# Grouping the products of the state steps and the attention by shape, and a new order for both

## The chip, the cores and the metric

One core of a Trainium2 chip. The metric is the device time of one execution in microseconds, the median of three runs. PE is TensorE, DVE is VectorE, ACT is ScalarE, POOL is GpSimd, SP is SyncE (here it only issues DMAs). PE's granted clock is 2.4 GHz where the profile shows 1.00 and 1.2 GHz where it shows 0.50.

## What the kernel computes

Two residual layers over 512 tokens of 1024 values. The change lies in the mixer of layer 0, which has eight heads of RWKV-7 and eight heads of stick-breaking attention, all 64 wide:

```
def step(S, inp):                                   # RWKV-7, one token
    r_t, w_t, k_t, v_t, a_t, b_t = inp
    sa = jnp.einsum('bhvk,bhk->bhv', S, a_t)
    S = S * w_t[:, :, None, :] + sa[..., None] * b_t[:, :, None, :] + v_t[..., None] * k_t[:, :, None, :]
    return S, jnp.einsum('bhvk,bhk->bhv', S, r_t)
...
for blk in range(t_len // SB_BLOCK):                # attention, 128 queries at a time
    z = jnp.einsum('bhqd,bhkd->bhqk', q[:, :, q0:end], k[:, :, :end]).astype(jnp.float32) * scale
    log_1m_beta = jnp.where(causal, jax.nn.log_sigmoid(-z), 0.0)
    after = lax.cumsum(log_1m_beta, axis=3, reverse=True) - log_1m_beta
    att = jnp.where(causal, jnp.exp(jax.nn.log_sigmoid(z) + after), 0.0)
    outs.append(jnp.einsum('bhqk,bhkd->bhqd', att.astype(v.dtype), v[:, :, :end]))
```

Before it comes the input projection, behind it the output projection, a mixture of 16 experts, layer 1 and another mixture.

## The kernel before, in words

The projections leave everything on the chip, then `values` prepares the RWKV part and the stage of this change begins: the state steps and the attention, woven into each other on PE, ACT and DVE. Two heads form a pair, 128 partitions, so there are four pairs in either part.

**The steps.** The 512 tokens are cut into 8 chunks of 64, and `step(c)` carries the state over one chunk for all pairs at once. It is a chain: `p1` multiplies the old state (L612), `d1` adds to it on DVE (L615), `p2` multiplies by a 128x128 inverse (L621), `a2` copies the result out of PSUM in two halves on ACT (L625), `p3` makes the new state (L630), which `d3` scales on DVE (L634, L635), and `p4` makes the output (L641, L643), which `a4` copies out (L646). The chain to the next step goes p2, a2, p3, d3, p1, d1. In `p1` and `p2` a product has 128 weight columns and 64 moving columns, one for each pair. In `p4` each pair has two products with all 128 rows and 64 columns of weights (L641) and two, for the old state, with 64 rows and 64 columns (L643), in turns.

**The attention.** A pair's 8 query blocks are packed into 5 units of 512 columns (`attend(k)`, pair k // 5, unit k % 5). A unit goes through `z` (scores on PE, L755, and a mask added as a product of an identity with a triangle of -1e30, L756), `a1` to `a3` on ACT (Abs, Exp, Ln), `d1` (DVE, L772), `d2` (running sums on DVE, one for each query block, L779), `d3` (DVE, scores less sums, L782), `t` (four transposes on PE, L786), `a4` (Exp on ACT, L790) and, for three of the five, `av` (weights times values, L804). Scores of units 1 to 4 are three products of split numbers (high x high, low x high, high x low) over a head's 64 rows; a unit of one head uses one half of PE's rows. `cut_qk` makes the split for the next pair, on ACT and POOL (L296, L297).

**What sets the order.** `even` gives each part a time from the tables STEP, UNIT, OUT and SPLIT, plus 2 * ITER = 16.4 for each pair, sorts the parts and issues them in that order; PE, ACT and DVE run their instructions in it, each engine by itself, with semaphores between. The tables are numbers of a plan, not times of the chip.

```
at = p * 2 * ITER
parts = [(at + t, f) for t, f in zip(UNIT[j], (z, a1, a2, a3, d1, d2, d3, t, a4, av))]
...
for _, f in sorted(parts, key=lambda x: x[0]):
    f()
```

Behind the stage comes `a_out` (16 products of 128x512 for the RWKV heads: L663, L671, L681, L682), then `out_proj`, whose weights and residual rows SP loads during the stage (L820, L951) as buffers come free.

Of the kernel before, what the change touches and what calls it, by code (L numbers as in the profile page):

```python
# [12 lines left out]
AF = mybir.ActivationFunctionType  # L13
OP = mybir.AluOpType
# [4 lines left out]
T = 512  # L19
# [24 lines left out]


ITER = 8.2
STEP = (dict(p1=1.45, d1=1.90, p2=2.59, a2=5.24, p3=5.37, d3=5.86, p4=10.90, a4=17.57),
        dict(p1=7.47, d1=8.81, p2=9.34, a2=10.12, p3=12.64, d3=14.66, p4=14.62, a4=18.80))
UNIT = ((0.00, 1.87, 4.48, 5.31, 5.68, 6.60, 6.64, 8.13, 9.59, 20.86),
# [4 lines left out]
OUT = 27.10, 37.12  # L54
SPLIT = 12.74


class Arena:
# [100 lines left out]
class Kern:  # L159
# [180 lines left out]
    def consts_even(self):  # L340
        nc, ar = self.nc, self.ar

        self.bo = ar.get(128)
        self.bo64 = ar.get(128)
        for b, v in ((self.bo, 1.0), (self.bo64, 1.0 / 64)):
            nc.gpsimd.memset(b.f(), 0.0)
            for s in range(2):
                nc.gpsimd.memset(b.f()[s * 64:s * 64 + 64, s * 64:s * 64 + 64], v)

        self.cm = ar.get(128)  # L350
        nc.gpsimd.memset(self.cm.f(), 1.0)
        for s in range(2):
            v = self.cm.f()[s * 64:s * 64 + 64]
            nc.gpsimd.affine_select(v[:, 0:64], v[:, 0:64], [[1, 64]], OP.is_gt, 0.0, base=0, channel_multiplier=-1)
            nc.gpsimd.affine_select(v[:, 64:128], v[:, 64:128], [[1, 64]], OP.is_ge, 0.0, base=0, channel_multiplier=-1)

        self.atc = ar.get(128)
        self.identb, self.late = self.atc.b(2, 128)[:, 0], self.atc.b(2, 128)[:, 1]
        nc.gpsimd.tensor_copy(self.identb, self.ident)
        nc.gpsimd.memset(self.late, 0.0)  # L360
        nc.gpsimd.affine_select(self.late, self.late, [[-1, 128]], OP.is_gt, -1e30, base=0, channel_multiplier=1)

        self.sm = ar.get(T)
        nc.gpsimd.memset(self.sm.f(), 1.0)
        nc.gpsimd.memset(self.sm.f(8, 64)[:, :, 0:1], 0.0)
# [226 lines left out]
    def step(self, c):  # L592


        nc, ar = self.nc, self.ar
        UV, AR = self.UV.f(8, 4, 2, 64), self.AR.f(4, 8, 3, 64)
        XI, RV, BT, MR = self.AMa.f(4, 8, 128), self.RV.f(4, 8, 64), self.BT.f(4, 8, 128), self.AMr.f(4, 8, 2, 64)
        S, old = [self.S[(c + i) % 2].f(4, 64) for i in range(2)]
        R1 = self.R1.f(4, 64)
        both = lambda a: a.rearrange("p s v -> p (s v)")  # L600
        q = [slice(s * 64, s * 64 + 64) for s in range(2)]
        pairs = [(p, s) for p in range(4) for s in range(2)]
        B = {}
# [12 lines left out]

        def p2():
            b = bank(2)
            rhs = R1 if c else RV[:, :, c]
            for p in range(4):  # L620
                nc.tensor.matmul(b[:, p], XI[:, p, c], rhs[:, p], start=True, stop=True)  # L621

        def a2():
            for s in range(2):
                nc.scalar.activation(UV[q[s], c, :, s], B[2][q[s]], AF.Copy)  # L625

        def p3():
            b = bank(3)
            for p, s in pairs:
                nc.tensor.matmul(b[q[s], p], BT[:, p, c, q[s]], UV[:, c, p, s], start=True, stop=True)  # L630

        def d3():
            if c:
                nc.vector.tensor_tensor(S, B[3], old, OP.add)  # L634
            nc.vector.tensor_tensor(S, S if c else B[3], self.LC.f(4, 8)[:, :, c:c + 1].to_broadcast([128, 4, 64]), OP.mult)  # L635

        def p4():
            b = bank(4)
            for p in range(4):
                for s in range(2):  # L640
                    nc.tensor.matmul(b[q[s], p], UV[:, c, p, s], MR[:, p, c, s], start=True, stop=not c)  # L641
                for s in range(2 if c else 0):
                    nc.tensor.matmul(b[q[s], p], old[q[s], p], AR[q[s], p, c, 2], start=False, stop=True, tile_position=(s * 64, s * 64))  # L643

        def a4():
            nc.scalar.activation(AR[:, :, c, 2], B[4], AF.Copy)  # L646

        parts = dict(p1=p1, d1=d1, p2=p2, a2=a2, p3=p3, d3=d3, p4=p4, a4=a4)
        skip = ("p1", "d1") if not c else ("p3", "d3") if c == 7 else ()
        return [(c // 2 * 2 * ITER + STEP[c % 2][n], f) for n, f in parts.items() if n not in skip]  # L650

# [79 lines left out]
    def attend(self, k):  # L731


        nc = self.nc
        p, j = divmod(k, 5)


        unit = ([(0, 1, 0), (1, 1, 256)], [(0, 3, 0)], [(1, 3, 0)], [(0, 2, 0), (0, 0, 384)], [(1, 2, 0), (1, 0, 384)])[j]
        N = 512
        B = {}  # L740

        def z():
            z = self.bank(("pj", "at")[k % 2])
            for s, qb, c in unit:
                hs, n = slice(s * 64, s * 64 + 64), qb * 128 + 128
                terms = [(self.QK[p].f(2, T), self.QK[p].f(2, T))]
                if not j:

                    hs, terms = slice(0, 128), [(self.QZ.f(2, 1, 128)[:, s], self.QK[p].f(2, T))]
                elif qb:  # L750
                    h, l = self.whi.bufs[p % 2].r(2, T), self.wlo.bufs[p % 2].r(2, T)
                    terms = [(h, h), (l, h), (h, l)]
                q = slice(qb * 128, n) if j else slice(0, 128)
                for i, (a, b) in enumerate(terms):
                    nc.tensor.matmul(z[:, c:c + n], a[hs, 0, q], b[hs, 1, 0:n], start=not i, stop=i == len(terms) - 1)  # L755
                nc.tensor.matmul(z[:, c + n - 128:c + n], self.identb, self.late, start=False, stop=True, skip_group_check=True)  # L756
            if not j and p < 3:
                self.beside(p + 1)
            B["z"], B["s"] = z, self.spq.next().f()


        def a1():
            nc.scalar.activation(B["s"], B["z"], AF.Abs)

        def a2():
# [3 lines left out]
            self.after(nc.scalar.activation(B["s"], B["s"], AF.Ln, bias=self.eps[:, 2:3]))  # L769

        def d1():
            nc.vector.scalar_tensor_tensor(B["s"], B["z"], 0.0, B["s"], OP.max, OP.add)  # L772


        def d2():
            for s, qb, c in unit:
                n = qb * 128 + 128
                v = _back(B["s"][:, c:c + n])
                nc.vector.tensor_tensor_scan(v, self.eps[:, 2:3].to_broadcast([128, n]), v, 0.0, OP.mult, OP.add)  # L779

        def d3():
            nc.vector.tensor_tensor(B["s"], B["z"], B["s"], OP.subtract)  # L782

        def t():
            for i in range(0, N, 128):
# [1 line left out]

        def a4():
            w = self.rsr.next().f()
            self.after(nc.scalar.activation(w, B["z"], AF.Exp))  # L790
            self.w[k] = w, unit

        def av():
# [11 lines left out]
                                     self.VT[p].f(4, 128)[:, kb, s * 64:s * 64 + 64], w, start=kb == 0, stop=kb == qb)  # L805

        at = p * 2 * ITER
        parts = [(at + t, f) for t, f in zip(UNIT[j], (z, a1, a2, a3, d1, d2, d3, t, a4, av))]
        if not j and p < 3:
            parts.append((at + SPLIT, lambda: self.cut_qk(p + 1)))  # L810
        if j == 4:
            parts += [(at + t, f) for t, f in zip(OUT, self.out_in(4 + p, lambda: self.o))]
        return parts
# [90 lines left out]
    def even(self):  # L904
        nc, ar, I = self.nc, self.ar, self.I
# [43 lines left out]
        x = I["x"].rearrange("b (t p) d -> p (b t) d", p=128)  # L949
# [724 lines left out]
```

## Time and profile before

| | us |
|---|---|
| median of 3 runs (1259.72 to 1261.07) | 1260.58 |
| the profiled execution, device time | 1263.75 |
| its span in the profile | 1262.0 |
| PE busy over the span | 1195.3 |
| DVE, ACT, POOL busy | 1027.3, 800.2, 486.4 |

The busy time of PE is modelled, so that 95% says only that PE seldom stands without an instruction. The trace numbers microseconds from the start of the span; the stage of this change runs from 250.91, when the first `p2` begins, to 338.35, when the last `av` ends.

### The profile page before, as it was taken

How to read it: one execution, taken by the hardware profiler on the slowest of the kernel's cores; microseconds unless marked ns; L12 is line 12 of the kernel's file. 1: busy time of each engine (PE TensorE's matmuls, PEld its weight loads, DVE VectorE, ACT ScalarE, POOL GpSimd, SP SyncE). 2: the span in 40 equal slices, each digit the busy share in tenths (PEclk: the TensorE clock that was granted, in tenths of full speed). 3: DMA queues.
4: the chain of work that ended last, by engine and by line, in shares of the span. 5: the costliest groups of instructions: out<-in, count | busy, mean ns of one | idle time of the engine just before them, and what ended most of it. 6: DMA issues, size and time to landing. Idle time of an engine off the chain costs nothing. (4 is left out here: it accounts for less than half of the span.)

```text
span 1262.0 us, 18000 instructions
## 1 busy us (share of the span) xinstructions
PE 1195.3 (95%) x6602; PEld 880.3 (70%) x6603; DVE 1027.3 (81%) x1316; ACT 800.2 (63%) x1071; POOL 486.4 (39%) x321
## 2 busy tenths in 40 slices
PE   6999998999999799999999899999997999999997
PEld 5777765877678477777777676677775777777764
DVE  4387899567776899999998665599657999999985
ACT  6533332367744588888888564475445888888883
POOL 8043200201011246667775301120113466667753
PEclk9999999979999899999999999999998999999998
DMA  6312221001776889999997532256678999999964
GB/s 167 84 50 67 67 67 34 2 18 43 258 245 232 311 293 361 356 346 357 351 365 265 155 87 67 68 174 239 221 247 277 327 367 369 350 345 347 352 223 145
DMA packets 152390, 274.46 MB, mean 217 GB/s; under 512 B 8171, under 2 KB 59052, under 8 KB 152294
## 3 DMA queue, kind: packets, MB, share of 16 engines
q1 hardware_dynamic: 142438, 247.85, 57.1%
q0 software_dynamic: 7840, 18.04, 6.1%
q10 hardware_dynamic: 2016, 7.34, 1.4%
q8 instruction: 54, 0.88, 0.3%
q14 instruction: 42, 0.34, 0.1%
HBM read 258.80 MB, written 22.28 MB: 223 GB/s over the span
## 5 line engine op out<-in xcount | busy, mean ns | idle before, releaser
L296 ACT ACTIVATE R<-A 128x1024 fp32r<-128x1024 f32 (+1 forms) x451 | 473.2, 1053 | 206.3 <-PE ps_pj L1350 68.0
L297 DVE TENSOR_TENSOR R<-A,R 128x1024 fp32r<-128x1024 f32 (+1 forms) x362 | 493.7, 1397 | 77.9 <-ACT R L296 73.9
L297 POOL TENSOR_TENSOR R<-A,R 128x1024 fp32r<-128x1024 f32 x89 | 257.1, 2889 | 292.7 <-ACT R L296 288.6
L1351 PE MATMUL ps_pj<-R 128*96 128x512 f32 x512 | 205.6, 401 | 9.9 <-DVE R L297 9.9
L1349 PE MATMUL ps_pj<-R 128*96 128x512 f32 x512 | 205.9, 402 | 0.0
L1350 PE MATMUL ps_pj<-R 128*96 128x512 f32 x512 | 204.0, 398 | 0.0
L324 PE MATMUL ps_pj<-R 128*128 128x512 f32 x296 | 120.9, 408 | 10.0 <-DVE A L709 9.2
L326 PE MATMUL ps_pj<-R 128*128 128x512 f32 x296 | 119.5, 404 | 3.5 <-DVE R L297 3.5
L325 PE MATMUL ps_pj<-R 128*128 128x512 f32 x296 | 121.2, 409 | 0.0
L1351 PEld LDWEIGHTS ps_pj<-R 128*96 128x96 f32 x512 | 84.1, 164 | 47.1 <-DVE R L297 10.8
L1350 PEld LDWEIGHTS ps_pj<-R 128*96 128x96 f32 x512 | 84.3, 165 | 35.7 <-DVE R L297 0.4
L1376 PE MATMUL ps_at<-R 128*96 128x512 f32 x256 | 103.8, 407 | 4.9 <-PEq L1571 1.8
L1349 PEld LDWEIGHTS ps_pj<-R 128*96 128x96 f32 x512 | 84.3, 165 | 34.0
L1378 PE MATMUL ps_at<-R 128*96 128x512 f32 x256 | 101.7, 397 | 0.0
L1377 PE MATMUL ps_at<-R 128*96 128x512 f32 x256 | 101.6, 397 | 0.0
L324 PEld LDWEIGHTS ps_pj<-R 128*128 128x128 f32 x296 | 56.2, 190 | 27.5 <-DVE A L709 11.2
L326 PEld LDWEIGHTS ps_pj<-R 128*128 128x128 f32 x296 | 56.0, 189 | 20.8 <-DVE R L297 5.6
L1385 POOL DMA_INDIRECT YD<-A x30 | 67.3, 2242 | 4.8 <-issue 2.4
L325 PEld LDWEIGHTS ps_pj<-R 128*128 128x128 f32 x296 | 56.3, 190 | 15.6 <-issue 4.7
L1152 POOL TENSOR_TENSOR A<-A 128x1024 f32<-128x1024 f32 x6 | 16.2, 2715 | 127.1 <-DVE A L858 87.5
L1254 DVE TENSOR_TENSOR A<-A 128x384 bf16<-128x384 f32 x32 | 60.0, 1885 | 0.0
L297 DVE TENSOR_TENSOR R<-ps_rw,R 128x384 fp32r<-128x384 f32 x92 | 47.7, 542 | 12.1 <-ACT R L296 12.0
(445 smaller groups left out, 2069.3 us busy)
## 6 DMA issues: line engine op xcount, KB each, us to landing
A<-in_exp_w_up_dram SPq DMA_DIRECT2D x61, 1024.0 KB
A<-in_exp_w_down_dram SPq DMA_DIRECT2D x61, 1024.0 KB
A<-in_exp_w_gate_dram SPq DMA_DIRECT2D x59, 1024.0 KB
A<-in_w_in_even_dram SPq DMA_DIRECT2D x27, 512.0 KB
A<-in_w_in_odd_dram SPq DMA_DIRECT2D x20, 512.0 KB
S<-in_exp_w_gate_dram SPq DMA_DIRECT2D x5, 1024.0 KB
A<-in_w_out_odd_dram SPq DMA_DIRECT2D x10, 512.0 KB
A<-in_x_dram SPq DMA_DIRECT2D x8, 512.0 KB
```

The source lines that it names most:

```text
L296: a = self.nc.scalar.activation(hi, src, AF.Copy)
L297: return a, (eng or self.nc.vector).tensor_tensor(lo, src, hi.bitcast(F32), OP.subtract)
L324: nc.tensor.matmul(p[0:n], hi[:, k], Hh[:, k], start=k == 0, stop=False)
L325: nc.tensor.matmul(p[0:n], hi[:, k], Hl[:, k], start=False, stop=False)
L326: nc.tensor.matmul(p[0:n], lo[:, k], Hh[:, k], start=False, stop=k == KD - 1)
L1349: self.nc.tensor.matmul(b, xh[:, k], hi, start=k == 0, stop=False)
L1350: self.nc.tensor.matmul(b, xl[:, k], hi, start=False, stop=False)
L1351: self.nc.tensor.matmul(b, xh[:, k], lo, start=False, stop=k == KD - 1)
L1376: nc.tensor.matmul(yb[n], hh[:, k], hi[:, cs], start=k == 0, stop=False)
L1377: nc.tensor.matmul(yb[n], hl[:, k], hi[:, cs], start=False, stop=False)
L1378: nc.tensor.matmul(yb[n], hh[:, k], lo[:, cs], start=False, stop=k == 3)
L1385: self.nc.gpsimd.indirect_dma_start(out=self.YD[l][:, :], out_offset=bass.IndirectOffsetOnAxis(ap=ix[0:SL], axis=0), in_=y.rearrange("p a ...
```

## The change

- `p1` and `p2`: each pair's product with 128 weight columns becomes two with 64, one for each head, written to the upper or the lower 64 partitions.
- `p4`: first the eight products of L641 for all pairs, then the eight of L643.
- `a2`: the second half is copied by DVE instead of ACT.
- `z`: the two heads' units with the same query blocks (1 and 2, 3 and 4) are issued as one part into two PSUM banks, one product of either head by turns; block 0 takes three split products too instead of one. The masks of a bank are one product, and the masked score is -2**100.
- `d1`, `d2`, `d3`: `d1` takes min and a reversed subtraction; one running sum goes over all of a unit's columns and adds the scores as it goes, reading them from PSUM; `d3` is gone, and `a4` takes exp of the negative. A masked score in a row's next block swamps what was summed before it, and the added FAR takes it out again.
- All tables are new; `cut_qk` comes earlier, `p1` and `p2` of the even steps ahead of their pair's scores.

```
-STEP = (dict(p1=1.45, d1=1.90, p2=2.59, a2=5.24, p3=5.37, d3=5.86, p4=10.90, a4=17.57),
+STEP = (dict(p1=-2.79, d1=-1.08, p2=-0.60, a2=2.34, p3=4.56, d3=5.76, p4=10.94, a4=12.34),
...
         def p1():
-            for p in range(4):
-                nc.tensor.matmul(b[:, p], both(AR[:, p, c, 0:2]), old[:, p], start=True, stop=True)
+            for p, s in pairs:
+                nc.tensor.matmul(b[q[s], p], AR[:, p, c, s], old[:, p], start=True, stop=True)
         def p2():
-            for p in range(4):
-                nc.tensor.matmul(b[:, p], XI[:, p, c], rhs[:, p], start=True, stop=True)
+            for p, s in pairs:
+                nc.tensor.matmul(b[q[s], p], XI[:, p, c, q[s]], rhs[:, p], start=True, stop=True)
         def a2():
-            for s in range(2):
-                nc.scalar.activation(UV[q[s], c, :, s], B[2][q[s]], AF.Copy)
+            nc.scalar.activation(UV[q[0], c, :, 0], B[2][q[0]], AF.Copy)
+            nc.vector.tensor_copy(UV[q[1], c, :, 1], B[2][q[1]])
         def p4():
-            for p in range(4):
-                for s in range(2):
-                    nc.tensor.matmul(b[q[s], p], UV[:, c, p, s], MR[:, p, c, s], start=True, stop=not c)
-                for s in range(2 if c else 0):
-                    nc.tensor.matmul(b[q[s], p], old[q[s], p], AR[q[s], p, c, 2], start=False, stop=True, tile_position=(s * 64, s * 64))
+            for p, s in pairs:
+                nc.tensor.matmul(b[q[s], p], UV[:, c, p, s], MR[:, p, c, s], start=not p, stop=not c, skip_group_check=True)
+            for p, s in pairs if c else ():
+                nc.tensor.matmul(b[q[s], p], old[q[s], p], AR[q[s], p, c, 2], start=False, stop=True, tile_position=(s * 64, s * 64), skip_group_check=True)
...
         def z():
+            if j:
+                z = [self.bank(("pj", "at")[i % 2]) for i in (k, k + 1)]
+                h, l = self.whi.bufs[p % 2].r(2, T), self.wlo.bufs[p % 2].r(2, T)
+                for x, (_, qb, c) in enumerate(unit):
+                    q, n = slice(qb * 128, qb * 128 + 128), qb * 128 + 128
+                    for i, (a, b) in enumerate(((h, h), (l, h), (h, l))):
+                        for s in range(2):
+                            hs = slice(s * 64, s * 64 + 64)
+                            nc.tensor.matmul(z[s][:, c:c + n], a[hs, 0, q], b[hs, 1, 0:n], start=not x and not i, stop=False, skip_group_check=True)
...
         def d1():
-            nc.vector.scalar_tensor_tensor(B["s"], B["z"], 0.0, B["s"], OP.max, OP.add)
+            nc.vector.scalar_tensor_tensor(B["s"], B["z"], 0.0, B["s"], OP.min, OP.subtract, reverse1=True)
         def d2():
-            for s, qb, c in unit:
-                n = qb * 128 + 128
-                v = _back(B["s"][:, c:c + n])
-                nc.vector.tensor_tensor_scan(v, self.eps[:, 2:3].to_broadcast([128, n]), v, 0.0, OP.mult, OP.add)
-        def d3():
-            nc.vector.tensor_tensor(B["s"], B["z"], B["s"], OP.subtract)
+            v = _back(B["s"][:, 0:N - 1])
+            nc.vector.tensor_tensor_scan(v, _back(B["z"][:, 1:N]), v, FAR, OP.add, OP.add)
```

What this makes of PE's order in the second half of the stage, first at the scores of units 1 and 2. Before (R are the split numbers, ps_at and ps_pj the banks of the units, S the masks and values):

```order
L755 MATMUL ps_at<-R 128x512 x3
L756 LDWEIGHTS S
L756 MATMUL ps_at<-S 128x128
L804 MATMUL ps_o<-A,S 64x128 x4
L786 MATMUL ps_at<-A 128x128 x4
L630 MATMUL ps_rw<-A 64x64 x8
L755 MATMUL ps_pj<-R 128x512 x3
L756 LDWEIGHTS S
L756 MATMUL ps_pj<-S 128x128
```

And in the changed kernel:

```order
L754 MATMUL ps_pj<-R 128x512
L754 MATMUL ps_at<-R 128x512
L754 MATMUL ps_pj<-R 128x512
L754 MATMUL ps_at<-R 128x512
L754 MATMUL ps_pj<-R 128x512
L754 MATMUL ps_at<-R 128x512
L771 LDWEIGHTS S
L771 MATMUL ps_pj<-S 128x128
L771 LDWEIGHTS S
L771 MATMUL ps_at<-S 128x128
L630 MATMUL ps_rw<-A 64x64 x8
```

The second head's scores have moved up beside the first's, and both masks stand behind them. PE at the outputs of the steps, before (L641 and L643 are `p4`, L630 is `p3`, L786 the transposes):

```order
L641 MATMUL ps_rw<-A 64x64 x2
L643 MATMUL ps_rw<-A 64x64 x2
L630 MATMUL ps_rw<-A 64x64 x8
L786 MATMUL ps_at<-A 128x128 x4
L641 MATMUL ps_rw<-A 64x64 x2
L643 MATMUL ps_rw<-A 64x64 x2
```

And in the changed kernel (L797 are the transposes, L621 `p2`, L612 `p1`):

```order
L621 MATMUL ps_rw<-A 64x64 x8
L641 MATMUL ps_rw<-A 64x64 x8
L643 MATMUL ps_rw<-A 64x64 x8
L797 MATMUL ps_at<-A 128x128 x4
L630 MATMUL ps_rw<-A 64x64 x8
L797 MATMUL ps_pj<-A 128x128 x4
L641 MATMUL ps_rw<-A 64x64 x8
L643 MATMUL ps_rw<-A 64x64 x8
L612 MATMUL ps_rw<-A 64x64 x8
```

Each `p4` is two runs of eight instead of eight runs of two, and `p1` and `p2` have eight products of 64 columns. DVE in the same region, before (L772 is `d1`, L779 `d2`, printed as SCALAR_TENSOR_TENSOR, L782 `d3`):

```order
L634 TENSOR_TENSOR A<-ps_rw,A 128x256
L635 TENSOR_TENSOR A<-A,S 128x256
L779 SCALAR_TENSOR_TENSOR A<-A 128x256 x2
L782 TENSOR_TENSOR A<-ps_pj,A 128x512
L615 TENSOR_TENSOR A<-ps_rw,A 128x256
L772 SCALAR_TENSOR_TENSOR A<-ps_at,A 128x512
L779 SCALAR_TENSOR_TENSOR A<-A 128x512
```

And in the changed kernel (L787 is `d1`, L793 `d2`, L625 the half of `a2`):

```order
L634 TENSOR_TENSOR A<-ps_rw,A 128x256
L635 TENSOR_TENSOR A<-A,S 128x256
L793 SCALAR_TENSOR_TENSOR A<-ps_at,A 128x511
L787 SCALAR_TENSOR_TENSOR A<-ps_pj,A 128x512
L615 TENSOR_TENSOR A<-ps_rw,A 128x256
L793 SCALAR_TENSOR_TENSOR A<-ps_pj,A 128x511
L625 COPY A<-ps_rw 64x4x64
L787 SCALAR_TENSOR_TENSOR A<-ps_at,A 128x512
```

`d3` has gone, a sum is one instruction, and the copy of `a2` stands between a sum and the next `d1`.

## Rows read from the trace of the kernel before

**Rows 1.** Windows of the stage: us, busy PE, PEld, DVE, ACT, POOL; PEclk; DMA share; GB/s

```profile
250.91:273.98 23.07, 22.89 (x159) 18.04 (x158) 15.99 (x25) 13.64 (x25) 3.45 (x4) 0.64 0.08 24
273.98:294.66 20.68, 20.68 (x218) 16.14 (x218) 14.92 (x25) 15.21 (x29) 2.94 (x3) 0.99 0.09 25
294.66:315.13 20.47, 20.47 (x218) 15.92 (x217) 16.07 (x26) 15.34 (x29) 2.37 (x1) 1.00 0.13 39
315.13:338.35 23.22, 23.22 (x238) 17.21 (x236) 18.10 (x36) 16.63 (x31) 1.23 (x3) 1.00 0.70 232
338.35:350.05 11.70, 11.70 (x27) 5.07 (x28) 9.10 (x15) 9.16 (x15) 0.91 (x3) 1.00 0.91 315
...
257.30:274.40 17.10, 17.10 (x113) 13.91 (x113) 12.32 (x18) 8.79 (x16) 2.93 (x3) 0.50 0.11 32
```

**Rows 2.** Who waited for whom, 235 to 350: us in total, times, longest

```profile
ACT A L763 <- PE ps_at L756: 7.9, 4, 4.7
DVE A L615 <- PE ps_rw L612: 7.3, 7, 3.4
```

**Rows 3.** Timeline of PE at p4, p3 and a transpose: start, us, what

```profile
286.44 0.34 PE L641 MATMUL ps_rw<-A 128*64 128x64 f32 x4
...
288.55 0.69 PE L630 MATMUL ps_rw<-A 128*64 128x64 f32 x16
289.17 0.65 PE L786 MATMUL ps_pj<-A 128*128 128x128 f32 x4
```

**Rows 4.** Timeline of PE at p1 and at the scores

```profile
292.99 1.06 PE L612 MATMUL ps_rw<-A 128*128 128x64 f32 x8
293.88 0.60 PE L786 MATMUL ps_at<-A 128*128 128x128 f32 x4
...
295.70 0.96 PE L755 MATMUL ps_at<-R 64*128 64x512 f32 x3
296.59 0.23 PE L756 MATMUL ps_at<-S 128*128 128x128 bf16 x1
...
299.59 0.79 PE L755 MATMUL ps_at<-R 64*128 64x384 f32 x3
...
300.95 1.06 PE L612 MATMUL ps_rw<-A 128*128 128x64 f32 x8
```

**Rows 5.** Timeline of PE in an earlier stage: two row halves by turns, and one

```profile
77.08 1.16 PE L485 MATMUL ps_rw<-A 64*128 64x128 f32 x16
...
148.29 1.13 PE L485 MATMUL ps_rw<-A 64*128 64x128 f32 x8 [0.41 <-DVE A L491]
```

**Rows 6.** Groups of DVE and ACT instructions, 294.66 to 315.13, by form

```profile
L779 DVE TENSOR_TENSOR_SCAN A<-A 128x512 f32<-128x512 f32 x2 | 2.4, 1221 | 0.0
L782 DVE TENSOR_TENSOR A<-ps_at,A 128x512 f32<-128x512 f32 x3 | 2.1, 685 | 0.0
...
L634 DVE TENSOR_TENSOR A<-ps_rw,A 128x256 f32<-128x256 f32 x2 | 0.8, 424 | 2.2 <-PE ps_rw L630 2.2
...
L625 ACT ACTIVATE A<-ps_rw 64x256 f32<-64x256 f32 x4 | 1.5, 376 | 0.0
```

**Rows 7.** Another running sum on DVE, whole execution, by form

```profile
L425 DVE TENSOR_TENSOR_SCAN S<-A 128x512 f32<-128x512 f32 x4 | 6.1, 1526 | 4.1 <-issue 4.1
```

**Rows 8.** A DVE copy like the moved half, 235 to 350

```profile
L587 DVE COPY A<-ps_rw 64x256 f32<-64x256 f32 x8 | 3.4, 428 | 1.6 <-ACT A L586 1.5
```

**Rows 9.** Timeline: a_out on PE in the tail, and SP's load of residual rows

```profile
332.09 0.33 SPq L951 DMA_DIRECT2D A<-in_x_dram  x1
...
333.13 1.88 PE L663 MATMUL ps_rw<-A 128*128 128x512 f32 x4
```

More of the change, by code (lines that the diff above doesn't have):

```diff
@@ L46 @@
 ITER = 8.2
-STEP = (dict(p1=1.45, d1=1.90, p2=2.59, a2=5.24, p3=5.37, d3=5.86, p4=10.90, a4=17.57),
-        dict(p1=7.47, d1=8.81, p2=9.34, a2=10.12, p3=12.64, d3=14.66, p4=14.62, a4=18.80))
-UNIT = ((0.00, 1.87, 4.48, 5.31, 5.68, 6.60, 6.64, 8.13, 9.59, 20.86),
[4 rows of a table removed]
-OUT = 27.10, 37.12
-SPLIT = 12.74
+STEP = (dict(p1=-2.79, d1=-1.08, p2=-0.60, a2=2.34, p3=4.56, d3=5.76, p4=10.94, a4=12.34),
+        dict(p1=6.50, d1=7.25, p2=10.12, a2=10.45, p3=12.48, d3=12.59, p4=12.86, a4=19.57))
+UNIT = (dict(z=-1.52, a1=-0.63, a2=1.23, a3=1.62, d1=3.40, d2=3.63, t=6.35, a4=7.04, av=15.18),
+        dict(z=3.09, a1=3.93, a2=5.35, a3=6.11, d1=6.47, d2=8.15, t=12.47, a4=12.58),
+        dict(a1=6.61, a2=7.18, a3=8.01, d1=9.71, d2=12.16, t=12.74, a4=12.82, av=21.09),
+        dict(z=7.62, a1=8.27, a2=8.38, a3=10.60, d1=12.38, d2=12.84, t=13.92, a4=14.19),
+        dict(a1=10.69, a2=11.58, a3=12.16, d1=14.20, d2=16.95, t=16.98, a4=19.49, av=23.90))
+OUT = 23.91, 24.81
+SPLIT = -3.19
+FAR = 2.0 ** 100
 class Arena:
@@ L360, in consts_even @@
         nc.gpsimd.memset(self.late, 0.0)
-        nc.gpsimd.affine_select(self.late, self.late, [[-1, 128]], OP.is_gt, -1e30, base=0, channel_multiplier=1)
+        nc.gpsimd.affine_select(self.late, self.late, [[-1, 128]], OP.is_gt, -FAR, base=0, channel_multiplier=1)
         self.sm = ar.get(T)
@@ L599, in step @@
         R1 = self.R1.f(4, 64)
-        both = lambda a: a.rearrange("p s v -> p (s v)")
         q = [slice(s * 64, s * 64 + 64) for s in range(2)]
@@ L735, in attend @@
         p, j = divmod(k, 5)
-        unit = ([(0, 1, 0), (1, 1, 256)], [(0, 3, 0)], [(1, 3, 0)], [(0, 2, 0), (0, 0, 384)], [(1, 2, 0), (1, 0, 384)])[j]
+        of = lambda j: ([(0, 1, 0), (1, 1, 256)], [(0, 3, 0)], [(1, 3, 0)], [(0, 2, 0), (0, 0, 384)], [(1, 2, 0), (1, 0, 384)])[j]
+        unit = of(j)
         N = 512
@@ L742, in z @@
         def z():
-            z = self.bank(("pj", "at")[k % 2])
-            for s, qb, c in unit:
[L745 to L756, printed above, removed]
@@ L757, in z @@
-            if not j and p < 3:
-                self.beside(p + 1)
-            B["z"], B["s"] = z, self.spq.next().f()
+            qk = self.QK[p].f(2, T)
+            if j:
[7 more added lines that the diff above has]
+                            nc.tensor.matmul(z[s][:, c:c + n], a[hs, 0, q], b[hs, 1, 0:n], start=not x and not i, stop=False, skip_group_check=True)
+                late = [b[:, N - 128 * len(unit):] for b in z]
+            else:
+                z = [self.bank(("pj", "at")[k % 2])]
+                for s, qb, c in unit:
+                    n = qb * 128 + 128
+                    nc.tensor.matmul(z[0][:, c:c + n], self.QZ.f(2, 128)[:, s], qk[:, 1, 0:n], start=not s, stop=False, skip_group_check=True)
+                late = [z[0].rearrange("p (a n) -> p a n", a=2)[:, :, 128:256]]
+                if p < 3:
+                    self.beside(p + 1)
@@ L762, in a1 @@
+            for b in late:
+                n = b.shape[-1] // 128 if j else 2
+                if j:
+                    b = b.rearrange("p (a n) -> p a n", a=n)
+                m = self.late.rearrange("p (a n) -> p a n", a=1).to_broadcast([128, n, 128])
+                nc.tensor.matmul(b, self.identb, m, start=False, stop=True, skip_group_check=True)
+            for i, b in enumerate(z):
+                self.z[k + i] = b
         def a1():
+            B["z"], B["s"] = self.z.pop(k), self.spq.next().f()
@@ L771, in d1 @@
         def d1():
-            nc.vector.scalar_tensor_tensor(B["s"], B["z"], 0.0, B["s"], OP.max, OP.add)
+            nc.vector.scalar_tensor_tensor(B["s"], B["z"], 0.0, B["s"], OP.min, OP.subtract, reverse1=True)
         def d2():
-            for s, qb, c in unit:
-                n = qb * 128 + 128
-                v = _back(B["s"][:, c:c + n])
-                nc.vector.tensor_tensor_scan(v, self.eps[:, 2:3].to_broadcast([128, n]), v, 0.0, OP.mult, OP.add)
-        def d3():
-            nc.vector.tensor_tensor(B["s"], B["z"], B["s"], OP.subtract)
+            v = _back(B["s"][:, 0:N - 1])
+            nc.vector.tensor_tensor_scan(v, _back(B["z"][:, 1:N]), v, FAR, OP.add, OP.add)
         def t():
@@ L789, in a4 @@
             w = self.rsr.next().f()
-            self.after(nc.scalar.activation(w, B["z"], AF.Exp))
+            self.after(nc.scalar.activation(w, B["z"], AF.Exp, scale=-1.0))
             self.w[k] = w, unit
@@ L807, in attend @@
         at = p * 2 * ITER
-        parts = [(at + t, f) for t, f in zip(UNIT[j], (z, a1, a2, a3, d1, d2, d3, t, a4, av))]
+        parts = dict(z=z, a1=a1, a2=a2, a3=a3, d1=d1, d2=d2, t=t, a4=a4, av=av)
+        parts = [(at + x, parts[n]) for n, x in UNIT[j].items()]
         if not j and p < 3:
@@ L933, in even @@
         self.wraw.free()
-        self.spq, self.rsr, self.w = Ring(ar, 2, T), Ring(ar, 4, T), {}
+        self.spq, self.rsr, self.w, self.z = Ring(ar, 2, T), Ring(ar, 4, T), {}, {}
         own = list(self.spq.bufs)
```

4 rows, old and new, of the table UNIT are left out of this document.

## The prediction

> **What bounds the kernel now.** I read the windows first, cut at the `p2` of steps 0, 2, 4 and 6, so that each holds one pair of the attention and two steps [rows 1]. The stage takes 87.4 us (250.91 to 338.35): 23.1 for the first pair, 20.7 and 20.5 for the next two, 23.2 for the last. PE is busy for the whole of each window, while DVE works 16.1 and ACT 15.3 of 20.5 us. That busy time is modelled, so I looked next at who waits for whom: the longest sums on the engines of the chain are ACT waiting for the last product of a unit's scores and DVE waiting for `p1` [rows 2], both waits for PE. So PE is the bound, and a product taken away there should shorten a pair until ACT or DVE is reached, some 5 us further down.
>
> The clock is the second thing in the windows. It was 1.00 in the last three and 0.64 in the first, because it stood at 0.50 from 257.30 to 274.40, 17.1 us in which PE issued 113 products and was never free [rows 1]. At full clock that stretch holds 8.55 us of work, so the first pair holds 23.1 - 8.55 = 14.5 us, fewer than the others because it has 159 products to their 218.
>
> **What a product costs.** All at full clock. The 16 products of `p4`, in eight runs of two, go from 286.44 to 288.55: 2.11 us; the eight of `p3`, one shape, take 0.62 until the transposes start [rows 3]. With s for a product and c for a change of shape, 16s + 8c = 2.11 and 8s + c = 0.62 give s = 0.059 and c = 0.145, an estimate from two rows. `p1`, four products with 128 weight columns, behind products as wide, takes 0.89 [rows 4]. Three score products of 512 columns take 0.89 (295.70 to 296.59), and a unit of 384 and 128 columns takes 1.36 from its start to the next product (299.59 to 300.95), of which 0.79 are scores [rows 4].
>
> **The change, part by part, for one pair (two steps).**
>
> PE, from 20.47:
> - *Fewer changes of shape.* I counted them in the two orders: 37 a pair before, 18 after, through `p4` and through `p1` and `p2` that now look like it. 19 x 0.145 = 2.76 less.
> - *`p1` and `p2`.* Eight products at 0.059 = 0.47 for 0.89, four times a pair: 1.68 less. The trace has no case of this very split; `p3`'s products have 64 weight columns too, so I take its price. The other bound is that it stays at 0.89.
> - *Scores by turns.* Two heads use the two halves of PE's rows, now one after the other into two banks. An earlier stage has both forms: 16 products on two row halves by turns took 1.16 us, eight on one half 1.13 [rows 5]. The second head was free there. So of the two joint parts one head's scores go: 0.89 less the change already counted, 0.75, and 0.79 in the same way 0.65, together 1.4. The other bound is nothing: L485's moving side is 128 columns and not 512, and two banks fill at once here.
> - Block 0's split adds four small products a pair, of 128 columns; the merged masks take some away. I set these against each other.
>
> PE comes to 20.47 - 2.76 - 1.68 - 1.4 = 14.6 us a pair; 16.0 if the turns save nothing.
>
> A rule speaks against the split. The Trainium skill ("TensorEngine Tiling (Array Packing)", Instruction Overhead) puts some 60 cycles on every matmul and warns against taking a tiling factor from a dimension that is already small. By it eight products for four, with 64 moving columns, would win nothing: `p1` and `p2` would keep 0.89, PE would come to 16.3, and the time below to about 1.6 us more. The rows of `p3` disagree, as eight such products took 0.62 us with the change of shape in it [rows 3].
>
> DVE, from 16.07: five `d3` go, 5 x 0.685 = 3.4. Two halves of `a2` come, at 0.43 each by the copy nearest in form [rows 8], 0.9 more. The sums cover the same columns; one of 512 took 1.22 from SBUF [rows 6], and another line's took 1.53 on the mean [rows 7]. The new one also reads PSUM; L634, which reads it, took 0.424 for 256 columns where `d3` took 0.685 for 512 [rows 6], so nothing shows a surcharge. I keep 1.22: 13.5 us a pair, and up to 15.0 at 1.53. What `d3` stood for on the path of a unit also goes.
>
> ACT, from 15.34: two halves of `a2` go, 2 x 0.376 [rows 6]: 14.6. The two halves no longer follow each other, which shortens the chain of a step by about 0.35, and that chain was not the bound.
>
> *The pace.* PE at 14.6 (or 16.0), ACT at 14.6 and DVE at 13.5 now lie so near each other that none can run without a gap; before, PE had 4 to 5 us of lead. I take 15.8: 1.2 of waits above the two lower figures, which is also 0.2 below PE without the overlap. Bounds 14.9, nearly none, and 17.5: PE at 16.0 and 1.5 of waits.
>
> **The sum for the stage.**
> - First pair: PE's 14.5 shrinks by 5.84 x 159/218 = 4.3 to 10.2 us of work. If the same 17.1 us run at half clock they do 8.55 of it, and 17.1 + 1.65 = 18.8 us. With no low stretch ACT sets it: 13.64 - 0.75 + some 1.4 until its first scores = 14.3. All of it low: 20.4.
> - Two pairs at 15.8: 31.6.
> - The last, with the run-out: 23.22 x 15.8 / 20.47 = 17.9.
> - `a_out`: before, two products of L663 were issued inside the tail (333.13, four records in 1.88 us [rows 9]); now all stand behind the last `av`. 1.8 more.
>
> 18.8 + 31.6 + 17.9 + 1.8 = 70.1 for 87.4: 17.3 less. The work behind the stage follows the last `av`. The residual rows and last weights are loaded as the step buffers come free (332.09 [rows 9]), which comes some 4 us later measured from the stage's end; `out_proj` begins 11.7 us behind it, in which DMA is at 0.91 [rows 1]. I count that as covered; uncovered it gives back up to 4.
>
> The profiled execution took 1263.75 (span 1262.0), 3.17 above the median of the runs, 1260.58. So 1246.4 for a profiled one, and **1243.3 us** for the median. 0.2% is 2.5 us, about what a measurement of this kernel can tell from no change.
>
> **The rivals.**
> - *The overlap or the split fails, or the order keeps its distances: 0.22.* The tables still give each pair 16.4, and PE at 16.0 to 16.3 with waits makes a pace of 16.4 to 17.5. Against it stand [rows 5]; for it, that ACT, DVE and PE are in each other's way. At 16.4 the stage is 18.8 + 32.8 + 18.6 + 1.8 = 72.0, time 1245; at 17.5 with the first pair at 20.4, 77.1, time 1250.
> - *The clock doesn't fall in the first pair: 0.12.* 14.3 for 18.8, so 1239; with a pace of 14.9, 1235. For it: only the first window has a stretch at 0.50. Against: nothing in the change speaks to what made it fall there.
> - *DVE becomes the bound: 0.05.* With 13.5 of work its sum must take 1.68 for DVE to reach 15.8, and neither row is there [rows 6, 7]. At 1.9 DVE works 16.9, the pace is about 17.5, the time 1249.
> - *Slower, because PE stays at 1.2 GHz through the stage: 0.05.* PE now has gaps, and the low stretch before came in the window with the fewest products [rows 1]. At half clock a pair takes 2 x 14.6 = 29.3 for 15.8, so a low microsecond costs 0.46. At full clock throughout the gain would be 87.4 - 65.6 = 21.8, eaten when 47 us are low, where 17 were. Low to the end: 20.4 + 58.6 + 33.2 + 3.6 = 116, time 1289. Against it: three of four windows stood at 1.00 with the transposes and masks between.
> - *No change: 0.03.* The gain of PE turns up as waits for ACT, with a pace near 20. ACT's 14.6 speaks against it.
>
> **How the numbers follow.** The forecast has 0.53 and lies at 1243.3, with 1240 to 1247 as its own range (pace 15 to 16.8). The range takes in both neighbours: 1235, where the clock holds and the pace is 14.9, to 1252, a pace of 17.5 with the first pair all low and some of the loads uncovered. Outside are part of the last two rivals and a greater give-back. Faster has the first four cases, 0.92; same 0.03; slower 0.05.
>
> **What would show it.** Right: cut at the same `p2`, the middle windows take about 15.8 us with PE no longer busy for all of it; eight products of `p2` and `p1` take about 0.47 and 16 of `p4` about 1.2; six score products of a joint unit take about as long as three did, 0.9 to 1.0; the running sums take 1.2 each, `d3` is gone and DVE waits for PE less than now; the low stretch ends within the first pair. Wrong: running sums of 1.7 or more, with PE waiting for DVE; six score products taking 1.8; PEclk at 0.5 in a second window; or the stage 17 us shorter while `out_proj` waits for its last weights.

## The result, and the profile after

The changed kernel takes 1241.78 us (median of 4 runs, 1239.99 to 1246.02) for 1260.82 before (median of 4, one more than stood there at the time of the forecast): ratio 0.9841, interval 0.9813 to 0.9869, so 19.0 us or 1.6% faster. Forecast were 1243.3 us and a range of 1235 to 1252. The profiled execution took 1241.28 us, its span 1239.6.

The windows of the stage after, cut at the first product of `p2` in steps 0, 2, 4 and 6, at the start of the last `av` product and at the first product of `out_proj` (columns as in [rows 1]):

```profile
249.55:264.13 14.58, 12.57 (x196) 9.86 (x197) 12.51 (x20) 12.13 (x22) 1.33 (x3) 1.00 0.14 37
264.13:280.07 15.94, 14.97 (x251) 12.05 (x249) 12.65 (x19) 14.34 (x27) 2.98 (x4) 1.00 0.12 35
280.07:296.00 15.93, 14.96 (x251) 12.04 (x249) 12.65 (x19) 13.38 (x26) 2.02 (x2) 1.00 0.17 51
296.00:313.34 17.34, 15.17 (x250) 12.24 (x246) 12.12 (x24) 13.88 (x27) 1.23 (x3) 1.00 0.69 247
313.34:326.98 13.64, 13.64 (x39) 6.05 (x35) 10.78 (x16) 9.61 (x16) 1.30 (x3) 1.00 0.94 332
```

The stage takes 63.8 us. Cut at the same instructions it took 87.1 before (251.02 to 338.07; the 87.4 above reach from the first weight load to the end of the last product). A middle pair takes 15.9 for 20.5, and PE is no longer busy for all of it: 15.0 us of work and 1.0 of gaps. The first pair has no stretch at 0.50, which before held 17.1 us [rows 1]. From the last `av` product to `out_proj` it is 13.6 us, for 12.0 before.

The timeline of PE after, at a joint unit's scores, and at `p2`, `p4`, the transposes and `p3` (columns as in [rows 3]):

```profile
265.29 0.49 PE L754 MATMUL ps_pj<-R 64*128 64x512 f32 x1
265.29 0.49 PE L754 MATMUL ps_at<-R 64*128 64x512 f32 x1
265.62 0.39 PE L754 MATMUL ps_pj<-R 64*128 64x512 f32 x1
...
266.18 0.23 PE L771 MATMUL ps_pj<-S 128*128 128x128 bf16 x1
...
272.23 0.69 PE L621 MATMUL ps_rw<-A 128*64 128x64 f32 x16
272.74 0.64 PE L641 MATMUL ps_rw<-A 128*64 128x64 f32 x16
273.31 0.68 PE L643 MATMUL ps_rw<-A 64*64 64x64 f32 x16
273.92 0.66 PE L797 MATMUL ps_pj<-A 128*128 128x128 f32 x4
```

Six products of 512 columns take 0.89 us (265.29 to 266.18), what three took before [rows 4]; the rows of the two banks start together. A product of plain fp32 numbers counts twice in these rows, so `p2`'s x16 are eight products; the split scores count once. `p2` takes 0.51 (272.23 to 272.74) and `p4` 1.18 (to 273.92) for 2.11 [rows 3].

Who waits for whom on PE, DVE and ACT through the stage after (us in total, times, longest):

```profile
DVE A L625 <- ACT A L624: 9.8, 8, 2.0
...
PE ps_at L797 <- DVE A L793: 2.7, 5, 0.9
PE ps_pj L797 <- DVE A L793: 2.6, 4, 1.2
...
DVE A L615 <- PE ps_rw L612: 1.3, 4, 0.5
...
PE ps_rw L612 <- DVE A L635: 0.6, 3, 0.2
```

DVE hardly waits for PE now. Its longest wait is a new one: its half of `a2` (L625) waits for ACT's half (L624). PE waits 5.3 us for running sums (L793) before it can transpose.

### The profile page after: what moved, and what is told of

Read it like the earlier page. It is cut to its first block, busy times and chain, and to the rows that moved or that the text cites. A ratio compares the mean times of both kernels' runs of the same rounds, so it can differ in the third digit from the quotient of the medians.

```text
span 1239.6 us, 18201 instructions
## 1 busy us (share of the span) xinstructions
PE 1166.2 (94%) x6718; PEld 861.0 (69%) x6719; DVE 1013.6 (82%) x1292; ACT 795.6 (64%) x1063; POOL 486.8 (39%) x321
## 5 line engine op out<-in xcount | busy, mean ns | idle before, releaser
L297 ACT ACTIVATE R<-A 128x1024 fp32r<-128x1024 f32 (+1 forms) x451 | 473.2, 1053 | 206.0 <-PE ps_pj L1362 67.2
L327 PEld LDWEIGHTS ps_pj<-R 128*128 128x128 f32 x296 | 56.4, 190 | 20.5 <-DVE R L298 5.7
L326 PEld LDWEIGHTS ps_pj<-R 128*128 128x128 f32 x296 | 56.5, 191 | 14.8 <-issue 4.1
L298 DVE TENSOR_TENSOR R<-ps_rw,R 128x384 fp32r<-128x384 f32 x92 | 47.7, 543 | 14.6 <-ACT R L297 14.5
```

The lines of the kernel that those rows point to most:

```text
L297: a = self.nc.scalar.activation(hi, src, AF.Copy)
L298: return a, (eng or self.nc.vector).tensor_tensor(lo, src, hi.bitcast(F32), OP.subtract)
L326: nc.tensor.matmul(p[0:n], hi[:, k], Hl[:, k], start=False, stop=False)
L327: nc.tensor.matmul(p[0:n], lo[:, k], Hh[:, k], start=False, stop=k == KD - 1)
```

## The experiments

All lengths below are windows of one profiled execution, cut as above. Where PE's clock stays at 1.00 the pairs repeat within 0.02 us in the two profiles of the changed kernel, which the whole time does not. So the stage is compared first, and the median beside it. A ratio compares with runs of the kernel before on the same chip; the medians come from several chips, on which the kernel before took 1260.8 to 1264.7. Two stages hold a stretch of low clock and are too long by it: old_order's in its first pair, a2_on_act's in its last.

| kernel | stage | pairs 2, 3 | PE in them | median us | ratio to before |
|---|---|---|---|---|---|
| before_again | 81.1 | 20.56, 20.47 | 20.5 | 1255.94, one run | |
| changed | 63.8 | 15.94, 15.93 | 15.0 | 1241.78 | 0.984 |
| after_again | 63.8 | 15.93, 15.93 | 15.0 | 1243.12, one run | |
| fwd_products | 74.8 | 18.79, 18.65 | 17.8 | 1257.52 | 0.990 to 0.998 |
| old_order | 79.6 | 18.61, 19.36 | 15.6 | 1259.72 | 0.994 to 0.998 |
| wide_p1p2 | 66.3 | 16.67, 16.67 | 16.3 | 1246.76 | 0.985 to 0.993 |
| p4_turns | 67.9 | 17.23, 17.22 | 16.6 | 1249.60 | 0.988 to 0.995 |
| z_heads_apart | 63.8 | 15.94, 15.95 | 15.0 | 1242.82 | 0.982 to 0.989 |
| z_mask_between | 66.6 | 16.70, 16.69 | 16.7 | 1245.81 | 0.982 to 0.987 |
| sums_apart | 73.8 | 18.24, 18.24 | 14.9 | 1252.42 | 0.991 to 0.996 |
| a2_on_act | 63.2 | 15.27, 15.27 | 15.1 | 1242.49 | 0.982 to 0.989 |
| a2_on_dve | 60.1 | 14.83, 14.83 | 14.7 | 1240.94 | 0.982 to 0.988 |
| a2_dve_first | 58.9 | 14.75, 14.74 | 14.6 | 1238.99 | 0.978 to 0.983 |

### The clock: both kernels once more

> The kernel before, profiled once more, for the clock. In the first profile the stage of the change took 87.4 us and its first pair 23.1, with PE at 0.50 for 17.1 us. Theory A (the low stretch belongs to this kernel's work): again 15 to 18 us at 0.50 within the first pair, stage 86 to 89 us. Theory B (it comes and goes from run to run): no such stretch, the first pair 14 to 16 us, stage 79 to 81.

> The changed kernel, profiled once more, for the clock. In its first profile the stage took 63.8 us, all of it at 1.00. Theory A (with the change PE's clock holds there): again 1.00 throughout and 63 to 65 us. Theory B (it comes and goes from run to run): a stretch of 3 to 17 us at 0.50 in the first pair and a stage of 65 to 69 us.

The windows of before_again:

```profile
249.79:267.06 17.27, 16.27 (x158) 12.31 (x157) 14.60 (x24) 13.82 (x26) 3.74 (x4) 1.00 0.11 32
267.06:287.62 20.56, 20.56 (x216) 16.01 (x217) 15.70 (x25) 14.90 (x28) 2.94 (x3) 1.00 0.09 26
...
308.09:330.92 22.83, 22.83 (x235) 16.99 (x234) 18.00 (x36) 16.52 (x31) 1.23 (x3) 1.00 0.68 230
```

Theory B for the kernel before: this time no low stretch, and a first pair of 17.3 us for 23.1 [rows 1], though 14 to 16 were expected. The changed kernel shows 1.00 in both profiles; that its clock holds there in every run is not shown. So at full clock the stage goes from 81.1 to 63.8, 17.3 us; the stretch at 0.50 cost the first profile another 5.9 (87.1 less 81.1).

The same products can now be compared at both clocks, first within the stretch at 0.50, then in before_again at 1.00 (L641 begins `p4`, L612 is `p1`):

```profile
257.31 1.06 PE L786 MATMUL ps_pj<-A 128*128 128x128 f32 x4
...
265.31 0.48 PE L641 MATMUL ps_rw<-A 128*64 128x64 f32 x4
...
268.59 1.22 PE L755 MATMUL ps_at<-A 128*128 128x256 f32 x2
...
270.78 1.91 PE L612 MATMUL ps_rw<-A 128*128 128x64 f32 x8
272.48 1.06 PE L786 MATMUL ps_pj<-A 128*128 128x128 f32 x4
```

```profile
256.08 0.61 PE L786 MATMUL ps_pj<-A 128*128 128x128 f32 x4
...
260.92 0.34 PE L641 MATMUL ps_rw<-A 128*64 128x64 f32 x4
...
263.03 0.70 PE L755 MATMUL ps_at<-A 128*128 128x256 f32 x2
...
264.16 1.06 PE L612 MATMUL ps_rw<-A 128*128 128x64 f32 x8
265.06 0.61 PE L786 MATMUL ps_pj<-A 128*128 128x128 f32 x4
```

`p4` took 3.28 us at 0.50 for 2.11 at 1.00, 1.55 times as long; `p1` 1.70 for 0.90, 1.9 times; the whole row of products from the first line to the last 15.17 for 8.98, 1.69 times. So the stretch at half clock held more work than half its length.

### The product forms alone, and the order alone

> The kernel before with the three product forms of the change alone: p1 and p2 in eight products of 64 weight columns, p4 in two runs of eight; its tables, scores, sums and copies as before. Theory A (PE is the bound and the terms are priced right): 12 changes of shape fewer x 0.145 + 1.68 = 3.4 us less a pair, pace 17.0 to 17.5, time 10 to 14 us under the kernel before. Theory B (the old order holds its distances, or the split wins nothing): pace 19 to 20.5, time at most 5 us less.

Its edits are those of `p1`, `p2` and `p4` in the diff above, put into the kernel before. It lies between the theories: PE's work fell by 2.7 us a pair (forecast 3.4), and PE stood still for 0.9. The stage is 6.3 us shorter than in before_again, the median 6.4 below 1263.96, that of the kernel before on the same chip.

> The changed kernel with the tables of the kernel before (its d3 times dropped; the joint scores of units 1 and 2 at 5.40 and those of 3 and 4 at 9.62, a1 of unit 3 at 9.70, since banks come free only then). Theory A (the work per pair sets the pace, and the new order adds what keeps PE fed): PE's work stays 15.0 a pair, waits grow, pace 16.5 to 18, time 2 to 8 us above the changed kernel's 1241.8. Theory B (the order is worth nothing): within 2 us of it.

```
-STEP = (dict(p1=-2.79, d1=-1.08, p2=-0.60, a2=2.34, p3=4.56, d3=5.76, p4=10.94, a4=12.34),
+STEP = (dict(p1=1.45, d1=1.90, p2=2.59, a2=5.24, p3=5.37, d3=5.86, p4=10.90, a4=17.57),
...
-        dict(z=3.09, a1=3.93, a2=5.35, a3=6.11, d1=6.47, d2=8.15, t=12.47, a4=12.58),
+        dict(z=5.40, a1=6.01, a2=6.04, a3=6.37, d1=9.31, d2=9.58, t=13.06, a4=15.52),
```

Its windows, and who waits in pairs 2 and 3:

```profile
253.38:273.44 20.06, 16.68 (x189) 12.80 (x189) 13.20 (x20) 12.38 (x23) 3.46 (x4) 0.74 0.10 27
273.44:292.05 18.61, 15.66 (x249) 12.48 (x248) 13.24 (x19) 14.39 (x28) 2.93 (x3) 1.00 0.11 30
292.05:311.41 19.36, 15.57 (x249) 12.38 (x249) 14.24 (x20) 14.22 (x27) 2.35 (x1) 1.00 0.14 42
```

```profile
PE ps_pj L761 <- ACT A L801: 1.4, 1, 1.4
PE ps_at L761 <- ACT A L801: 1.4, 1, 1.4
...
DVE A L625 <- ACT A L624: 7.6, 3, 3.3
```

Theory A, but by far more than expected: pairs 2 and 3 are 6.1 us longer than the changed kernel's and the stage 15.8, where the time was to rise by 2 to 8; the median is only 4.2 below that of before on the same chip. Most of PE's savings are there (15.6 us of work a pair for 20.5), yet a pair takes 19.0 on the mean, so 3.4 us of it are gaps. PE waits for score banks that ACT has not read (L761 on L801), and DVE for ACT's half of `a2`. The first pair's clock was 0.74 here; pairs 2 and 3 stood at 1.00.

### One part undone at a time

> The changed kernel with p1 and p2 as before, four products of 128 weight columns. Theory A (the split is worth what the sum says): p1 and p2 take 0.9 for 0.5 us, PE's work goes from 15.0 to 16.5 a pair, pace 15.9 to 16.6 to 17.5, the stage 3 to 6 us longer. Theory B (eight small products for four win nothing): 0.5 us as before in the rows, or no change of the stage beyond 1 us.

```
 def p2():
-    for p, s in pairs:
-        nc.tensor.matmul(b[q[s], p], XI[:, p, c, q[s]], rhs[:, p], start=True, stop=True)
+    for p in range(4):
+        nc.tensor.matmul(b[:, p], XI[:, p, c], rhs[:, p], start=True, stop=True)
```

The same in `p1`. Theory A, though the stage, 2.5 us longer, stays just under its range. `p1` on PE's timeline, with what follows it:

```profile
274.81 1.08 PE L612 MATMUL ps_rw<-A 128*128 128x64 f32 x8 [0.21 <-DVE A L635]
275.82 0.88 PE L815 MATMUL ps_o<-A 128*64 128x128 f32 x12
```

1.01 us, a change of shape in it, for 0.51 of `p2` in eight products. PE's work rises by 1.35 a pair; 0.6 of that fills gaps, and the pair becomes 0.74 longer. So the split wins, against the rule as the prediction read it, and the rows of `p3` were the better guide. What is divided are the 128 weight columns, not the 64 moving ones; why eight such products take half the time of four was not tested.

> The changed kernel with p4 in eight runs of two products as before. Theory A (a change of shape costs 0.145): p4 takes 2.1 for 1.2 us, twice a pair, PE's work 16.7, the stage 3 to 7 us longer. Theory B (the changes cost nothing, or waits hide them): within 1 us.

The edit puts back the loops of `p4` as they stand with a minus in the diff above. Theory A: with `p4` in runs of two PE's work is 1.62 higher, 0.135 for each of the 12 changes of shape, a pair 1.29 longer, the stage 4.1.

> The changed kernel with the joint scores issued head by head: all of one head's products, then the other's, into the same two banks. Theory A (products on the two row halves overlap only by turns): six products of 512 columns take 1.8 for 0.9 us, PE's work rises by 1.4 to 1.6 a pair, the stage 2 to 6 us longer. Theory B (the halves overlap in any order, or the six are short for another reason): 0.9 to 1.1 again, the stage within 1 us.

```
-for i, (a, b) in enumerate(((h, h), (l, h), (h, l))):
-    for s in range(2):
+for s in range(2):
+    for i, (a, b) in enumerate(((h, h), (l, h), (h, l))):
```

Theory A fell. PE's timeline of z_heads_apart, in which the program, as built, issues all three products into `ps_pj` and then all three into `ps_at`:

```profile
270.16 0.49 PE L754 MATMUL ps_pj<-R 64*128 64x512 f32 x1
270.17 0.49 PE L754 MATMUL ps_at<-R 64*128 64x512 f32 x1
270.49 0.39 PE L754 MATMUL ps_pj<-R 64*128 64x512 f32 x1
270.50 0.39 PE L754 MATMUL ps_at<-R 64*128 64x512 f32 x1
...
271.06 0.23 PE L771 MATMUL ps_pj<-S 128*128 128x128 bf16 x1
```

The second head's first product starts 0.01 us after the first head's, ahead of two products issued before it, and the six take 0.90.

> The changed kernel with the joint scores issued head by head and the first head's mask between the two heads. Issued head by head without it, six products of 512 columns still took 0.9 us, and the stage 63.8 as before, so turns are not needed. Theory A (the two row halves run side by side as long as no product over all 128 rows stands between): now six products and a mask take 1.9 to 2.1 us, PE's work rises by 1.4 to 2.0 a pair (the overlap, and at most 4 changes of shape at 0.145), pace 16.3 to 17.5, the stage 2 to 6 us longer. Theory B (the six are short for another reason, and place in the order plays no part): 1.1 to 1.3 us, PE's work up by at most 0.6, the stage at most 2 us longer.

The added lines:

```
+for s in range(2):
+    for x, (_, qb, c) in enumerate(unit):
...
+            nc.tensor.matmul(z[s][:, c:c + n], a[hs, 0, q], b[hs, 1, 0:n], ...)
+    if not s:
+        mask(z[0][:, N - 128 * len(unit):])
```

```profile
271.42 0.96 PE L761 MATMUL ps_pj<-R 64*128 64x512 f32 x3
272.31 0.23 PE L748 MATMUL ps_pj<-S 128*128 128x128 bf16 x1
272.47 0.96 PE L761 MATMUL ps_at<-R 64*128 64x512 f32 x3
273.37 0.23 PE L748 MATMUL ps_at<-S 128*128 128x128 bf16 x1
```

Theory A. With one product over all 128 rows between them the heads run one after the other, 0.89 and 0.90 us. PE's work rises by 1.7 a pair; the pair becomes 0.76 longer, since 1.0 of it fills the gaps. The Trainium skill ("TensorEngine Tiling (Array Packing)", Key Properties) says that tiles work independently of each other and can run their products in parallel. The trace agrees, with six products in 0.90 us. What part the issue order plays these two runs show: 0.90 us head by head, 1.95 (271.42 to 273.37) with the mask between.

> The changed kernel with the running sums as before: one for each query block, from SBUF, d1 with max and add, and d3 (scores less sums) behind the sums; a4 takes the exponential of its plain input, the mask is -1e30. Theory A (without the saved d3 DVE would be the bound): DVE's work goes from 12.7 to about 16.5 a pair, pace 17 to 18, the stage 5 to 9 us longer. Theory B (PE hides it): within 2 us.

The sums and `d3`; `d1`, `a4` and the mask go back to their old form too:

```
-    v = _back(B["s"][:, 0:N - 1])
-    nc.vector.tensor_tensor_scan(v, _back(B["z"][:, 1:N]), v, FAR, OP.add, OP.add)
+    for s, qb, c in unit:
+        n = qb * 128 + 128
+        v = _back(B["s"][:, c:c + n])
+        nc.vector.tensor_tensor_scan(v, self.eps[:, 2:3].to_broadcast([128, n]), v, 0.0, OP.mult, OP.add)
+    nc.vector.tensor_tensor(B["s"], B["z"], B["s"], OP.subtract)
```

```profile
269.45:287.69 18.24, 14.88 (x252) 11.89 (x250) 16.79 (x28) 14.61 (x27) 3.56 (x4) 1.00 0.10 31
```

Theory A, slightly past its range: DVE's work 16.8 (forecast 16.5), PE's unchanged, a pair 2.3 longer, the stage 10.0. In these two pairs PE waits 6.2 us for the sums.

### Who copies `a2`

> The changed kernel with both halves of a2 on ACT, as before. In the profile of the changed kernel DVE's half waits for ACT's (9.8 us in eight steps). Theory A (the split gives no parallel work, since the second half starts only when the first is done): the stage within 1 us, DVE's wait goes to its next instruction. Theory B (moving the half to DVE relieved ACT and the chain): ACT at 15.1 of 15.9 us, the stage 2 to 4 us longer.

```
-nc.vector.tensor_copy(UV[q[1], c, :, 1], B[2][q[1]])
+nc.scalar.activation(UV[q[1], c, :, 1], B[2][q[1]], AF.Copy)
```

Better than either theory: a pair takes 15.27, 0.66 less than with the split. DVE's wait does go to its next instruction, as theory A has it: `d1` waits for ACT 6.6 us in pairs 2 and 3. Its last pair held a short stretch of low clock (0.91 on the mean, 18.6 us), so only its middle pairs are to be compared.

> The changed kernel with both halves of a2 on DVE. Theory A (DVE loses time behind ACT's late half, and the transposes wait for its sums, 5.3 us in the stage): the wait for ACT is gone, d1 and the sums come 0.5 to 1 earlier, the stage 1 to 4 us shorter. Theory B (the waits of PE for the sums come from the order): within 1 us; if DVE's 13.5 us of work come into the way, up to 2 longer.

The edit gives DVE the first half as well. Theory A at its upper end: a pair takes 14.83, the stage 60.1, with DVE at 13.5 us of work.

> The changed kernel with the two copies of a2 written in the other order: DVE's half first, then ACT's. Theory A (the second copy waits for the first by a semaphore between the engines, whichever is second): DVE's half waits for PE alone, ACT's half for DVE's; DVE is free earlier, and the stage comes between 60.1, both on DVE, and 63.8. Theory B (DVE's half came late for another reason, such as PSUM read by both): DVE's half still ends behind ACT's, the stage within 0.5 us of 63.8.

```
-nc.scalar.activation(UV[q[0], c, :, 0], B[2][q[0]], AF.Copy)
 nc.vector.tensor_copy(UV[q[1], c, :, 1], B[2][q[1]])
+nc.scalar.activation(UV[q[0], c, :, 0], B[2][q[0]], AF.Copy)
```

Theory A, and shorter than forecast: 58.9 us. DVE at such a step in the changed kernel, and then in a2_dve_first:

```profile
266.07 0.43 DVE L625 COPY A<-ps_rw 64x256 f32<-64x256 f32 x1 [1.99 <-ACT A L624]
266.53 0.69 DVE L787 SCALAR_TENSOR_TENSOR A<-ps_at,A 128x512 f32<-128x512 f32 x1
267.25 1.22 DVE L793 TENSOR_TENSOR_SCAN A<-ps_at,A 128x511 f32<-128x511 f32 x1
```

```profile
266.56 0.43 DVE L624 COPY A<-ps_rw 64x256 f32<-64x256 f32 x1 [0.75 <-PE ps_rw L621]
267.56 0.69 DVE L787 SCALAR_TENSOR_TENSOR A<-ps_at,A 128x512 f32<-128x512 f32 x1 [0.57 <-ACT A L784]
```

In the changed kernel `p2` was over at 264.70, when the transposes began, but ACT came to its half only at 265.68, behind a unit's `a3`, and DVE stood for 1.99 us. With the lines swapped DVE waits for PE alone, and ACT, which has other work at that time, is second: it waits once for DVE, 1.2 us in the whole stage, and PE waits for sums 1.4 us for 5.3. So the second copy waits for the first, whichever engine does it. The wait stands in the program: as built, in all eight steps the second copy carries a semaphore on the first, in both kernels. What asks for it was not tried (the two read one PSUM tile and write different partitions of another). The stage of this version is the shortest of all, 4.9 us under the changed kernel's. Its ratio to before is 0.9803 for 0.9841, and the two intervals overlap, so the whole time alone does not tell the two apart.

## Why the prediction was right, step by step

**The bound.** That PE was the bound holds: what took work from it made pairs shorter (fwd_products), and PE's work fell from 20.5 to 15.0 a pair, forecast 14.6. By the runs that undo one part: `p1` and `p2` 1.35 (forecast 1.68), `p4` 1.62 (12 changes of shape at 0.145: 1.74), the joint scores 1.7 (1.4 and the changes around them). PE's time is modelled: with the same products it reads 14.6 in a2_dve_first and 15.1 in a2_on_act, so 0.4 from the forecast is no more than the reading allows. In [rows 5] the prediction took records for products (x16 are eight products, x8 four); the two stand to each other as it says.

**The pace.** 15.93 for 15.8, and the gaps 1.0 for 1.2. What makes the gaps is named now: in pairs 2 and 3 of after_again PE waits 2.0 us, four times 0.4 before transposes for sums and twice 0.2 for `p1`; behind the sums stands DVE's wait for ACT's half of `a2`, without which pairs shrink to 14.8 (a2_on_dve).

**DVE.** 12.7 for 13.5; the sum of 511 columns took 1.22 reading PSUM, as one from SBUF did [rows 6]. Most of the 0.8 lies outside the prediction's terms: before, one of the two L635 in a pair ran beside POOL's half of `cut_qk` and took 1.14 us, the other 0.43; in the changed kernel POOL does that at another time, and in pairs 2 and 3 all take 0.43. The kernel before:

```profile
288.24 2.36 POOL L297 TENSOR_TENSOR R<-A,R 128x1024 fp32r<-128x1024 f32 x1 [16.93 <-ACT R L296]
...
289.74 1.14 DVE L635 TENSOR_TENSOR A<-A,S 128x256 f32<-128x256 f32 x1
...
299.11 0.43 DVE L635 TENSOR_TENSOR A<-A,S 128x256 f32<-128x256 f32 x1
```

The rival with DVE as the bound is out, but sums_apart shows how near it was: with `d3` kept, a pair takes 18.2.

**The term with the wrong sign.** I counted the split of `a2` as 0.35 us less on the chain of a step, hidden. It costs 0.66 a pair: the halves do follow each other, and DVE stands in between.

**The term that was missing.** The sum had none for the order; I let PE's savings pass on to the pair and gave the old distances only a rival's place. old_order shows that with the old tables they pass only in part: 19.0 for 15.9. Undoing the parts one at a time gives 0.74, 1.29, 0.76, 2.31 and 3.1 us a pair, 8.2 together, where the whole change gave 4.6. They don't add up, since the order is laid out for the parts, and the parts' gain needs the order.

**The first pair.** Here the forecast's case did not come; the rival "the clock doesn't fall" did: 14.58, which it had as 14.3, for 18.8. The step that failed is the working of 14.5 us for the first pair before: it took 17.27 at full clock. I had counted the stretch at 0.50 as work worth half its length. The same products took there only 1.55 to 1.9 times as long as at full clock, and at full clock the pair has 1.0 us in which PE stands. So its gain at full clock is 2.7 us (17.27 to 14.58), where the sum has 4.3; against the profile from which the sum started it is 8.5.

**Luck in the time.** That the time came out near the forecast, and not at that rival's 1239, is in part luck. At full clock the difference to the first product of `out_proj` is 15.7 us (93.1 to 77.4, before_again against the changed kernel), and these two executions, both with a mean clock of 0.982, differ by 14.7 (1255.94 and 1241.28). The median moved by 19.0. Of the 14 unprofiled runs beside before_again one has its clock and its time (0.982, 1255.86 us); the others have 0.970 to 0.980 and 1259.68 to 1267.95 us; the changed kernel's four have 0.975 to 0.982. So runs of the kernel before mostly hold some low clock; where, no trace shows. The 4 us above 14.7 may come from it, which the forecast had not worked out.

**The rest.** The tail took 17.3 for 17.9. `a_out` took 1.6 us more behind the stage at full clock, forecast 1.8. From there to the end the changed kernel takes 912.6 us, the two profiles of the kernel before 912.0 and 911.3: if the late loads cost anything, it is at most 1.4.

## What to carry to other kernels

Products that use one half of PE's rows belong side by side with those of the other half, with nothing over all rows between them; for runs of three, by turns or not was all the same. Products of one shape belong together too, at 0.135 us a change (p4_turns). When a copy is shared out between two engines, look whether the second half waits for the first, and if it does, give the first half to the engine that is free when the data come. And a saving on the bound engine reaches the time in full only when the order of the engines is laid out for it: here the old tables ate two thirds of a middle pair's gain. Before a stretch at half clock is counted as half its length, look for the same products in a run at full clock.

## What the runs showed of the hardware

- PE ran products of its two row halves side by side even when one half's were all issued first: six of 512 columns in 0.90 us, and 1.95 with one product over all rows between the halves.
- The same program had 17.1 us at half clock in the stage in one profile and none in another. The stretch cost 5.9 us, 0.35 for each us: the same products took 1.55 (`p4`) to 1.9 (`p1`) times as long at 0.50 as at 1.00, 1.69 times over 15.2 us of it.
- A running sum that adds a PSUM operand as it goes took 1.22 us for 511 columns, the same as one from SBUF without it.
- A DVE instruction on two SBUF operands of 128x256 (L635) took 1.14 us beside a POOL instruction on two SBUF operands (L297) and 0.43 apart from one.
